# Linear-attention output product as seven block products behind the attention, with the final product begun in part

## Chip, cores and metric

The kernel runs on one core of a Trainium2 chip. The metric is the device time of one execution in microseconds; 1779.88 is the median of three runs before the change (1779.48 to 1781.68). Engines are named as in the profile: PE is TensorE (PEld its weight loads), DVE VectorE, ACT ScalarE, POOL GpSimd, SP the queue from which the transfers are issued.

## What is computed

One layer of a streaming encoder, 1024 tokens of width 1024, float32. Cut to what matters here:

```
h = rms_norm(x, pre_mix_norm)
h_q, h_k, h_v, h_g, h_a, c_q, c_kv, k_pe = split(h @ w_in)
o   = rms_norm(gated_linear_attention(h_q, h_k, h_v, h_a)) * silu(h_g)
y_a = o @ w_o_gla                       # the output product of the change
y_b = mla(c_q, c_kv, k_pe) @ w_o_mla    # the merge product
g_a, g_b = split(sigmoid(h @ w_gate + b_gate))
mixed = (g_a * y_a + g_b * y_b) @ w_out # the final product
x = x + rms_norm(mixed, post_mix_norm)
x = x + rms_norm(swiglu_ffn(rms_norm(x, pre_ffn_norm)))
```

## The kernel before

Everything is kept transposed: features on the 128 partitions, tokens along the free dimension in two halves of 512. A matmul in float32 is done as three (`mm3`, L93 to L96): each operand is split into a high half (cast, ACT, L104) and the rest (subtraction, DVE, L105), and high x high, high x low and low x high are added in PSUM. Weights come through `wload`: a transfer into a raw buffer (12 of them), then the split into wh and wl (7 of each). Activations come through `load4`: a transfer into a small buffer (15 of 128x512, tag h), then the split into one large buffer (34 of 128x1024, tag u).

The large products (projections, merge, FFN) are made by `wino`, the Strassen-Winograd form: of the 2x2 blocks of both operands seven block products instead of eight, with sums of operand blocks ahead (`t_ops`, `spilled_ops` for activations, `prep` for weights) and sums of products behind. Of some groups the first product and the second are made early and the first is spilled (npre groups, p1D).

Order of the work around the change. The attention (`qk`, `pt`, `av`) runs head by head over four blocks of 256 queries: scores p_sc, softmax on DVE and ACT, transposes p_pt, split into th and tl, product p_av; the scores of one step stand before the transposes of the step before. In the last head, parts of `gla_out(0, ...)` stand between them: the output product y_a for the first half of the tokens, eight tiles of 24 matmuls each (p_wog), each multiplied by its gate (L909) and stored to maD. The rest of `gla_out(0)` is interleaved with `merge_ops`, which makes the merge operands from omD (seven sets of four, 28 large buffers; b11 and b21 by `half0_ops`). Then comes the merge (p_pre, p_wa, p_wb, four of its groups begun early), whose `merge_use` multiplies by the second gate, adds maD for the first half and stores to mgD. Then `half_out(0)`, the final product for the first half (p_wout); then `gla_out(1)`, the output product for the second half, with `merge1` adding mgD and making the operands mp; then `half_out(1)`; then the FFN (p_pre, p_wa, p_wb again). The norm chain of the first half (`chain0`, with `pre_ffn`) runs beside `gla_out(1)` and `half_out(1)` and makes the FFN's first operands.

The order is written out in Python by generators that are advanced step by step; within this the framework's scheduler places instructions on each engine by priority in program order, and each engine then runs its list in order. So the SP queue: a transfer that waits holds those behind it.

Of the kernel before, what the change touches and what calls it, by code (L numbers as in the profile page):

```python
# [14 lines left out]
F32 = mybir.dt.float32  # L15
# [49 lines left out]
def body(tc, a, out):  # L65
# [139 lines left out]
    ogD = dp.tile([8, P, 1024], F32, name="ogD")  # L205
    gaD = dp.tile([8, P, 1024], F32, name="gaD")
    maD = dp.tile([8, P, H2], F32, name="maD")
# [232 lines left out]
    def wino(ops, slot, groups, npre):  # L440
# [56 lines left out]
        def full(gi, d, nxt, side):  # L497
# [3 lines left out]
            def banks():  # L501
                if gi % 2:
# [112 lines left out]
    def down_sums():  # L615

        for p in range(4):
            for c in range(0, KH * P, H2):
# [9 lines left out]
                yield 1  # L628

# [195 lines left out]
    def og_use(m0, m1):  # L825
        o = {}

        def load(i):
            o[i] = Hf("o")
            dma(o[i], oD[(m0, m1)[i // 2]][:, HS[i % 2]])  # L830

        def use(i, src):
# [4 lines left out]
            dma(ogD[(m0, m1)[i // 2]][:, HS[i % 2]], t)  # L837
# [5 lines left out]
    hgroups += [("wg", m, m + 1, og_use(m, m + 1)) for m in range(0, 8, 2)]  # L843
# [11 lines left out]
    sums = down_sums()  # L855
    for hd in range(HEADS_A):
# [15 lines left out]
        for i in range(NT + 2):  # L872
            run(sgen)
            run(fill)
            if 1 <= i < 7:
# [23 lines left out]
    def gla_out(j, ogs, use):  # L899
        for m in range(8):  # L900
            w = wload(a["wog"][m])
            ga = Hf("ga")
            dma(ga, gaD[m][:, HS[j]])
            ps = B(name="p_wog")
            for kt in range(KD):
                mm3(ps, w[kt], ogs[kt], kt == 0, kt == KD - 1)
                if kt == 3:
                    yield 1
            dve.tensor_tensor(ga, ps, ga, op=ALU.mult)  # L909
            use(m, ga)  # L910
            yield 1
# [128 lines left out]


# [10 lines left out]
    for s, (hd, blk) in enumerate(steps):  # L1052
# [22 lines left out]
    mops = dict(b11=[], b21=[], b22=[], t1=[], t2=[], t3=[], t4=[])  # L1075
    def merge_ops():
        ptt = pt(pend[1], pend[2])
        yield 1
        av(pend[0], pend[1], ptt)
        yield 1  # L1080
        yield from spilled_ops(mops, omD)

    mgen = merge_ops()
    def half0_ops():
        for n, k0 in (("b11", 0), ("b21", 4)):
            for kt in range(k0, k0 + 4):
                mops[n].append(load4(omD[kt][:, HS[0]]))
                if kt % 2:
                    yield 1

    h0gen = half0_ops()
    for i, _ in enumerate(gout):
        run(mgen)
        if i >= 6:
            run(h0gen)
    finish(h0gen)

    def merge_use(m0, m1):

        def use(i, src):  # L1100
# [3 lines left out]
            if j == 0:  # L1104
                ma = Hf("ma")
                dma(ma, maD[m])
            dve.tensor_tensor(gb, src, gb, op=ALU.mult)
            if j == 0:
                dve.tensor_tensor(gb, gb, ma, op=ALU.add)
# [3 lines left out]
    early, rest, _ = wino(mops, 0, [("wom", m, m + 1, merge_use(m, m + 1)) for m in range(0, 8, 2)], 4)  # L1113
    for _ in early:
        run(mgen)
    finish(mgen)
    rest()

    def half_out(j, wname, acts, sl, nk, filler=None, mid=None):

        raw = [U([P, 2, H2], name="raw") for _ in range(4)]
        sq = Hf("sq")
        for m in range(8):
            ps = B(name="p_" + wname)
            for k0 in range(0, nk, 4):
                k1 = min(nk, k0 + 4)
                w = wload(a[wname][m][:, k0 * P:k1 * P])
                for kt in range(k0, k1):
                    mm3(ps, w[kt - k0], cols(acts[kt], sl), kt == 0, kt == nk - 1)
                if mid is not None:  # L1130
                    run(mid)
# [48 lines left out]
    ogs = []  # L1180
# [324 lines left out]
```

## Time and profile before

| what | value |
|---|---|
| median of 3 runs | 1779.88 us |
| profiled execution | 1780.31 us, span 1778.5 us |
| PE busy | 1733.6 us, 8818 matmuls |
| DVE busy | 1268.2 us |
| ACT busy | 809.9 us |
| SP queue | 303.88 MB, 51.1% of 16 engines |
| granted clock | 0.997 |

The time of the profiled execution is the span and what lies around it. Busy times add the spans of instructions, which overlap on PE and DVE; how often an instruction can follow another is read from starts. A row of the timeline or of the chain gives the start, the length, and how many were merged (x24); a row of waits gives who waited for whom, the sum, how often, and the longest.

### The profile page before, as it was taken

Reading aid. Unit: us, or ns where it says so; the run is one execution under the profiler, and the core shown is the slowest. Engines: PE = TensorE matmul, PEld = TensorE weight load, DVE = VectorE, ACT = ScalarE, POOL = GpSimd, SP = SyncE. Lnnn points to the kernel's source line nnn. Section 1 sums busy time; section 2 is a strip of 40 time slices with the busy share of each in tenths; the row PEclk is TensorE's granted clock in tenths of the full one; section 3 lists DMA queues with packets and bytes.
Section 4 is the critical chain, followed back from the end, with each engine's and each line's share of the span. In section 5 each row is a group of like instructions: output and inputs, shape, how many; then the busy total and the mean of one; then the engine's idle time right before and its main releaser. Section 6 shows DMA issues by size and latency. Waiting matters only on the chain.

```text
span 1778.5 us, 25162 instructions
## 1 busy us (share of the span) xinstructions
PE 1733.6 (97%) x8818; PEld 1465.0 (82%) x8818; DVE 1268.2 (71%) x2275; ACT 809.9 (46%) x1511; POOL 39.5 (2%) x49
## 2 busy tenths in 40 slices
PE   8999999999999999999999999999999999999997
PEld 6889998777788898998877788788888888878886
DVE  7676665796556788787697668677887866655666
ACT  5485445634344554555452545452322322454542
POOL 0100000000000000000000000000000000000001
PEclk9999999999999999999999999999999999999999
DMA  6356753785556211112487654735554523593665
GB/s 243 137 197 204 226 169 121 272 283 195 182 197 206 60 51 53 34 51 94 169 307 271 210 184 142 243 135 173 177 183 153 186 95 109 175 317 108 197 187 172
DMA packets 172591, 305.49 MB, mean 172 GB/s; under 512 B 20080, under 2 KB 39280, under 8 KB 172464
## 3 DMA queue, kind: packets, MB, share of 16 engines
q1 hardware_dynamic: 172464, 303.88, 51.1%
q8 instruction: 69, 1.13, 0.3%
q14 instruction: 58, 0.48, 0.1%
HBM read 212.32 MB, written 89.39 MB: 170 GB/s over the span
## 4 chain that ended last, share of the span: by engine, by line
PE 84%; DMA 5%; DVE 5%; ACT 3%; issue 2%; SPq 1%; POOL 0%; DVEq 0%; ACTq 0%; POOLq 0%
PE p_wb L96 15%; PE p_wa L96 14%; PE p_wfd L96 11%; PE p_pre L96 8%; PE p_v L96 5%; PE p_wog L96 5%; PE p_wout L96 5%; PE p_sc L96 4%; PE p_av L96 3%; PE p_q L96 2%; PE p_k L96 2%; PE p_wqn L96 2%; PE p_pt L1013 1%; PE p_nrm L96 1%; DMA cl<-crD 1%
## 5 line engine op out<-in xcount | busy, mean ns | idle before, releaser
L104 ACT CAST wh<-raw 128x512 fp32r<-128x512 f32 (+1 forms) x335 | 200.7, 603 | 373.4 <-PE p_wfd L96 98.5
L105 DVE TENSOR_TENSOR wl<-raw,wh 128x512 fp32r<-128x512 f32 (+1 forms) x335 | 220.5, 664 | 160.3 <-ACT wh L104 152.5
L96 PE MATMUL p_wa<-t,wh 128*128 128x512 f32 x640 | 201.1, 394 | 3.9 <-DVE u L520 3.9
L96 PE MATMUL p_wb<-t,wh 128*128 128x512 f32 x640 | 198.2, 390 | 1.3 <-ACT wh L104 1.3
L96 PE MATMUL p_wfd<-ld,wh 128*128 128x512 f32 (+1 forms) x660 | 193.1, 377 | 3.0 <-ACT raw L1411 1.4
L96 PEld LDWEIGHTS p_wa<-t,wh 128*128 128x128 f32 x640 | 118.8, 188 | 33.4 <-DVE u L520 8.8
L96 PEld LDWEIGHTS p_wfd<-ld,wh 128*128 128x128 f32 x660 | 120.8, 188 | 26.7 <-ACT raw L1411 1.8
L96 PEld LDWEIGHTS p_wb<-t,wh 128*128 128x128 f32 x640 | 120.4, 188 | 26.6 <-ACT wh L104 1.7
L96 PE MATMUL p_wb<-t,wl 128*128 128x512 f32 x320 | 124.8, 390 | 0.0
L96 PE MATMUL p_wa<-t,wl 128*128 128x512 f32 x320 | 124.4, 391 | 0.0
L96 PE MATMUL p_wfd<-ld,wl 128*128 128x512 f32 (+1 forms) x330 | 123.2, 375 | 0.0
L104 ACT CAST wh<-sa 128x512 fp32r<-128x512 f32 x80 | 48.5, 620 | 156.8 <-DVE sa L458 82.9
L96 PE MATMUL p_v<-wh,hn 128*128 128x256 f32 x512 | 99.2, 283 | 0.6 <-ACT cr L667 0.5
L104 ACT CAST wh<-sb 128x512 fp32r<-128x512 f32 x80 | 49.7, 621 | 99.6 <-PE p_wb L96 49.3
L96 PEld LDWEIGHTS p_v<-wh,hn 128*128 128x128 f32 x512 | 82.5, 191 | 3.8 <-ACT cr L667 1.0
L96 PE MATMUL p_wog<-ld,wh 128*128 128x512 f32 x256 | 80.4, 392 | 1.0 <-DVE ld L105 0.7
L96 PE MATMUL p_pre<-b,wh 128*128 128x512 f32 x256 | 79.4, 396 | 0.0
L105 DVE TENSOR_TENSOR ld<-ld,ld 128x512 fp32r<-128x512 f32 x109 | 70.4, 687 | 9.8 <-ACT ld L104 9.6
L96 PE MATMUL p_v<-wl,hn 128*128 128x256 f32 x256 | 72.4, 283 | 0.0
L104 ACT CAST ld<-ld 128x512 fp32r<-128x512 f32 x109 | 63.4, 618 | 19.4 <-DMA ld<-fD 6.5
L96 PEld LDWEIGHTS p_wfd<-ld,wl 128*128 128x128 f32 x330 | 62.1, 188 | 11.3
L96 PE MATMUL p_pre<-hn,wh 128*128 128x512 f32 x224 | 71.0, 397 | 0.3 <-ACT p L485 0.2
(349 smaller groups left out, 4063.8 us busy)
## 6 DMA issues: line engine op xcount, KB each, us to landing
ld<-fD SPq DMA_DIRECT2D x77, 256.0 KB, 4.2
raw<-in_wfd_dram SPq DMA_DIRECT2D x60, 256.0 KB, 2.9
raw<-in_wfg_dram SPq DMA_DIRECT2D x60, 256.0 KB, 3.7
raw<-in_wfu_dram SPq DMA_DIRECT2D x60, 256.0 KB, 3.0
raw<-in_wgate_dram SPq DMA_DIRECT2D x48, 256.0 KB, 3.9
fD<-sg SPq DMA_DIRECT2D x41, 256.0 KB, 2.1
p1D<-p SPq DMA_DIRECT2D x34, 256.0 KB, 3.2
p<-p1D SPq DMA_DIRECT2D x34, 256.0 KB, 3.8
```

The costliest lines, as they stand in the source:

```text
L96: pe.matmul(o, l, r, start=start, stop=stop, skip_group_check=skip)
L104: act.copy(h, src)
L105: dve.tensor_tensor(l, src, h.bitcast(F32), op=ALU.subtract)
L1013: pe.transpose(tp[:, jj, i * P:(i + 1) * P], prs[i][:, j * P:(j + 1) * P], ident)
```

## The change

Three arrays change: gD holds the seven operand sets of the output product, soD the sums of its weights, maD both token halves. `og_use` in the projection stage, now with feature blocks m and m+4 in a group, makes the operand sums beside the gated columns and stores all to gD. `out_sums`, run after `down_sums` in the scan's stage (eight steps per head instead of six), makes the weights' sums. `gla_out` becomes the seven products n = 0 to 6 over four tiles p each, with both token halves at once, and stands as a whole after the last head; the merge operands are made beside it from its seventh step on. The merge makes no product early (npre 0) and begins on the other banks of PSUM. `merge_use` adds maD for both halves. `half_out(0)` begins with the first four k of three tiles. The operands of `half_out(1)` are loaded from mgD during `half_out(0)`, and `chain0` runs beside `half_out(1)` alone.

```diff
+    def out_sums():
+        for p in range(4):
+            a11, a12, a21, a22 = [wraw(a["wog"][2 * p + i][:, HS[k]]) for i in range(2) for k in range(2)]
+            yield 1
+            dve.tensor_tensor(a22, a21, a22, op=ALU.add)
+            dve.tensor_tensor(a21, a11, a21, op=ALU.subtract)
+            dve.tensor_tensor(a11, a22, a11, op=ALU.subtract)
+            dve.tensor_tensor(a12, a12, a11, op=ALU.subtract)
+            for i, t in enumerate((a22, a11, a21, a12)):
+                dma(soD[i, p], t)
+            yield 1
...
-            dma(ogD[(m0, m1)[i // 2]][:, HS[i % 2]], t)
+            if i != 1:
+                dma(gD[(0, 1, 1, 6)[i], m0], t)
+            if i:
+                f[i] = t
+            if i == 1:
+                b11, b12, b21, b22 = [f.pop(k) for k in range(4)]
+                ta, tb = U([P, 2, H2], name="ta"), U([P, 2, H2], name="tb")
+                dve.tensor_tensor(ta[:, 1], b12, b11, op=ALU.subtract)
+                dve.tensor_tensor(tb[:, 0], b22, ta[:, 1], op=ALU.subtract)
+                dve.tensor_tensor(ta[:, 0], b22, b12, op=ALU.subtract)
+                dve.tensor_tensor(tb[:, 1], b21, tb[:, 0], op=ALU.subtract)
+                for k, x in ((2, tb[:, 0]), (3, ta[:, 0]), (4, ta[:, 1]), (5, tb[:, 1])):
+                    dma(gD[k, m0], x)
...
-            if 1 <= i < 7:
+            if 1 <= i < 9:
                 run(sums)
...
+        def use(p, i, src):
+            m, j = 2 * p + i // 2, i % 2
             ga = Hf("ga")
             dma(ga, gaD[m][:, HS[j]])
+            dve.tensor_tensor(ga, src, ga, op=ALU.mult)
+            dma(maD[m][:, HS[j]], ga)
...
+        for n in range(7):
+            ops, nxt = nxt, []
+            loader = out_set(n + 1, nxt) if n < 6 else iter(())
...
+            bank = x if n in (0, 1, 4, 6) else y
+            for p in range(4):
+                w = wload(weights(n, p))
+                for k in range(4):
+                    mm3(bank[p], w[k], ops[k], n in (0, 2, 4, 5) and k == 0, k == 3, n in (1, 3, 6))
+                run(loader)
+                yield 1
+                if n == 0:
+                    act.copy(p1[p], x[p])
+                elif n == 1:
+                    use(p, 0, x[p])
+                elif n == 2:
+                    dve.tensor_tensor(u2[p], y[p], p1[p], op=ALU.add)
...
+                else:
+                    dve.tensor_tensor(u2[p], x[p], u2[p], op=ALU.add)
+                    use(p, 1, u2[p])
+            finish(loader)
...
-        if hd == HEADS_B - 1:
-            if blk == 0:
-                ogs = [load4(ogD[kt][:, HS[0]]) for kt in range(8)]
-                gout = gla_out(0, ogs, lambda m, t: dma(maD[m], t))
-            run(gout, (0,1,2,2)[blk])
...
+        if hd == HEADS_B - 1:
+            run(oload)
...
+    for i, _ in enumerate(gla_out()):
+        if i == 1:
+            ptt = pt(pend[1], pend[2])
+        elif i == 2:
+            av(pend[0], pend[1], ptt)
+        elif i >= 6 and i % 2 == 0:
+            run(h0gen)
+            run(mgen)
+        elif i >= 6:
+            run(mgen)
...
-    early, rest, _ = wino(mops, 0, [("wom", m, m + 1, merge_use(m, m + 1)) for m in range(0, 8, 2)], 4)
+    _, rest, _ = wino(mops, 0, [("wom", m, m + 1, merge_use(m, m + 1)) for m in range(0, 8, 2)], 0, 1)
...
+            for i in range(3) if m == 0 and ahead else (m,) if m > 2 or not ahead else ():
+                part(i, 0)
+            part(m, 4)
...
-    for i, _ in enumerate(gla_out(1, ogs, merge1)):
-        if i % 2:
-            run(c0)
-    r1, s1 = half_out(1, "wout", mp, ALL, KD, None, c0)
+    def mid0():
+        while True:
+            for n in (1, 2, 1):
+                run(c0, n)
+                yield 1
+    r1, s1 = half_out(1, "wout", mp1, ALL, KD, None, mid0())
```

How the order moves. First place: PE in the last head, from the transposes of its first block of queries to the product with the values (p_pt transposes, p_av the product, p_wog the output product, p_sc the scores of a later block). Before:

```order
L1013 MATMUL p_pt_9240<-cst,pf_9098 128x128 x2
L96 MATMUL p_wog_9263<-ld_9140,wh_9251 128x512 x2
L96 MATMUL p_wog_9263<-ld_9140,wl_9252 128x512
...
L96 MATMUL p_wog_9263<-ld_9160,wh_9257 128x512
L96 MATMUL p_av_9276<-th_9245,v2h_8602 128x256
L96 MATMUL p_wog_9263<-ld_9160,wh_9257 128x512
```

and with the change:

```order
L1099 MATMUL p_pt_9314<-cst,pf_9207 128x128 x2
L96 MATMUL p_av_9323<-th_9319,v2h_8711 128x256
L96 MATMUL p_av_9323<-tl_9320,v2h_8711 128x256
L96 MATMUL p_av_9323<-th_9319,v2l_8712 128x256
...
L96 MATMUL p_sc_9338<-kp_6004,qs_8368 128x320
```

The thirteen matmuls of the output product that stood between the transposes and p_av are gone, and nothing stands in their place.

Second place: DVE where the merge operands are made (hb and t1 to t4: sums of merge operands and their low halves; ld: low halves of loaded operands; wl: low halves of weights; ga: gate multiplication; po: sums of products). Before, over the last tiles of the output product:

```order
L105 TENSOR_TENSOR wl_2211_9878<-raw_2209_9875,wh_2210_9877 128x512
L587 TENSOR_TENSOR t3_2161_9693<-hb_2152_9664,hb_2150_9660 128x512
L105 TENSOR_TENSOR wl_2214_9884<-raw_2212_9881,wh_2213_9883 128x512
L105 TENSOR_TENSOR b22_2162_9695<-hb_2152_9664,b22_2162_9695 128x512
L591 TENSOR_TENSOR hb_2150_9660<-hb_2150_9660,hb_2149_9658 128x512
L592 TENSOR_TENSOR hb_2152_9664<-hb_2152_9664,hb_2150_9660 128x512
L909 TENSOR_TENSOR ga_2159_9678<-p_wog_2160_9680,ga_2159_9678 128x512
```

and with the change, at the weights of the last tile of the fourth product (wl_2274):

```order
L986 TENSOR_TENSOR po_2126_9522<-p_wog_2197_9816,po_2126_9522 128x512
L593 TENSOR_TENSOR hb_2255_10018<-hb_2255_10018,hb_2253_10014 128x512
L105 TENSOR_TENSOR ld_2267_10070<-ld_2266_10068,ld_2267_10070 128x512
L597 TENSOR_TENSOR hb_2254_10016<-hb_2254_10016,hb_2255_10018 128x512
L105 TENSOR_TENSOR t2_2268_10075<-hb_2255_10018,t2_2268_10075 128x512
L105 TENSOR_TENSOR t3_2269_10078<-t3_2261_10044,t3_2269_10078 128x512
L105 TENSOR_TENSOR t1_2270_10081<-hb_2253_10014,t1_2270_10081 128x512
L105 TENSOR_TENSOR t4_2271_10085<-hb_2254_10016,t4_2271_10085 128x512
L105 TENSOR_TENSOR wl_2274_10092<-raw_2272_10089,wh_2273_10091 128x512
L105 TENSOR_TENSOR wl_2283_10124<-raw_2281_10121,wh_2282_10123 128x512
```

Before, weights for coming tiles stood ahead of most of the merge's work; now the weights of the fourth product's last tile stand behind that of three of its four row pairs, and with operand loads and sums of products between.

Third place: PE in the sixth product of the changed output product (four tiles p_wog_2195 to 2198; ld_2285, 2294, 2305, 2312 its four operands). Before, a tile ran through all its operands:

```order
L96 MATMUL p_wog_2160_9680<-ld_2026_9140,wh_2154_9668 128x512 x2
L96 MATMUL p_wog_2160_9680<-ld_2026_9140,wl_2155_9669 128x512
L96 MATMUL p_wog_2160_9680<-ld_2028_9145,wh_2154_9668 128x512 x2
L96 MATMUL p_wog_2160_9680<-ld_2028_9145,wl_2155_9669 128x512
L96 MATMUL p_wog_2160_9680<-ld_2030_9150,wh_2154_9668 128x512 x2
```

and with the change:

```order
L96 MATMUL p_wog_2197_9816<-ld_2294_10175,wl_2329_10316 128x512
L96 MATMUL p_wog_2198_9817<-ld_2285_10141,wh_2334_10343 128x512 x2
L96 MATMUL p_wog_2198_9817<-ld_2285_10141,wl_2335_10344 128x512
L96 MATMUL p_wog_2198_9817<-ld_2294_10175,wh_2334_10343 128x512 x2
L96 MATMUL p_wog_2198_9817<-ld_2294_10175,wl_2335_10344 128x512
L96 MATMUL p_wog_2195_9814<-ld_2305_10219,wh_2316_10259 128x512
L96 MATMUL p_wog_2196_9815<-ld_2305_10219,wh_2322_10287 128x512
```

All four tiles take the first two operands before any takes the third.

## Rows read from the trace of the kernel before

**Rows 1.** The page's head and its busy times.

```profile
span 1778.5 us, 25162 instructions
PE 1733.6 (97%) x8818; PEld 1465.0 (82%) x8818; DVE 1268.2 (71%) x2275; ACT 809.9 (46%) x1511; POOL 39.5 (2%) x49
```

**Rows 2.** Groups of instructions: matmuls of the output product; count, busy us, mean ns, idle before.

```profile
L96 PE MATMUL p_wog<-ld,wh 128*128 128x512 f32 x256 | 80.4, 392 | 1.0 <-DVE ld L105 0.7 <-DVE tl L105 0.3
...
L96 PE MATMUL p_wog<-ld,wl 128*128 128x512 f32 x128 | 50.1, 391 | 0.0
```

**Rows 3.** The chain that ended last, in order of time: start us, us, what.

```profile
856.31 1.20 PE p_pt L1013 x11
...
872.88 2.87 PE p_av L96 x24
875.75 20.86 PE p_wog L96 x92
...
990.23 39.30 PE p_wout L96 x171
```

**Rows 4.** PE's waits from 856.3 to 1000 us: total us, times, longest.

```profile
PE p_wa L96 <- DVE u L520: 1.4, 1, 1.4
PE p_wb L96 <- ACT wh L104: 1.3, 1, 1.3
PE p_wout L96 <- ACT ld L104: 1.2, 2, 1.0
PE p_pre L96 <- DVE wl L105: 1.2, 1, 1.2
PE p_pre L96 <- ACT p L485: 1.0, 2, 0.7
PE p_wout L96 <- DVE ld L105: 0.8, 1, 0.8
PE p_wog L96 <- DVE tl L105: 0.3, 1, 0.3
```

**Rows 5.** Busy time by stretch: us, PE, PEld, DVE, ACT, POOL, clock, DMA share, GB/s.

```profile
890.00:900.00 10.00, 10.00 (x46) 8.29 (x45) 9.83 (x18) 6.86 (x12) 0.00 (x0) 1.00 0.93 306
900.00:910.00 10.00, 8.84 (x40) 6.99 (x39) 8.98 (x15) 6.54 (x13) 0.00 (x0) 1.00 0.83 286
910.00:920.00 10.00, 9.73 (x43) 7.73 (x42) 10.00 (x18) 3.03 (x6) 0.00 (x0) 1.00 0.98 345
920.00:930.00 10.00, 8.01 (x34) 5.99 (x34) 9.05 (x16) 4.41 (x8) 0.00 (x0) 1.00 0.90 311
...
280.00:300.00 20.00, 19.14 (x107) 16.40 (x106) 10.31 (x19) 11.54 (x23) 0.70 (x1) 1.00 0.25 90
520.00:540.00 20.00, 20.00 (x93) 16.59 (x92) 12.50 (x19) 9.47 (x14) 0.72 (x1) 1.00 0.67 230
```

**Rows 6.** Timeline of DVE near 907 us: start us, us, instruction.

```profile
905.97 0.68 DVE L592 TENSOR_TENSOR hb<-hb,hb 128x512 f32<-128x512 f32 x1
...
908.98 0.69 DVE L105 TENSOR_TENSOR t<-hb,t 128x512 fp32r<-128x512 f32 x1
```

**Rows 7.** The page's costliest groups: the cast of a loaded operand.

```profile
L104 ACT CAST ld<-ld 128x512 fp32r<-128x512 f32 x109 | 63.4, 618 | 19.4 <-DMA ld<-fD 6.5
```

**Rows 8.** PE's waits from 564 to 1125 us: the attention products.

```profile
PE p_av L96 <- DVE tl L105: 1.7, 3, 0.8
```

**Rows 9.** Transfers issued from 870 to 990 us: count, KB, median us to landing.

```profile
hb<-omD SPq DMA_DIRECT2D x16, 256.0 KB, 5.0
```

**Rows 10.** Timeline of PE near 470 us: start us, us, instruction, idle before.

```profile
464.67 0.50 PE L96 MATMUL p_wa<-t,wh 128*128 128x512 f32 x1 [1.64 <-DVE u L520]
...
472.45 1.16 PE L96 MATMUL p_nrm<-cst,cl 128*128 128x2 f32 x8 [1.37 <-DVE cl L643]
473.47 1.20 PE L96 MATMUL p_wa<-t,wh 128*128 128x512 f32 x2
```

**Rows 11.** Busy time by stretch, as in rows 5, after these two gaps.

```profile
474.00:476.00 2.00, 2.00 (x6) 1.57 (x5) 1.94 (x4) 1.23 (x3) 0.97 (x1) 0.50 0.00 0
```

More of the change, by code (lines that the diff above doesn't have):

```diff
@@ L204, in body @@
     oD = dp.tile([8, P, 1024], F32, name="oD")
-    ogD = dp.tile([8, P, 1024], F32, name="ogD")
+    gD = dp.tile([7, 4, P, H2], F32, name="gD")
+    soD = dp.tile([4, 4, P, H2], F32, name="soD")
     gaD = dp.tile([8, P, 1024], F32, name="gaD")
-    maD = dp.tile([8, P, H2], F32, name="maD")
+    maD = dp.tile([8, P, 1024], F32, name="maD")
     mgD = dp.tile([2, 8, P, H2], F32, name="mgD")
@@ L825, in og_use @@
     def og_use(m0, m1):
-        o = {}
+        o, f = {}, {}
         def load(i):
@@ L830, in load @@
             dma(o[i], oD[(m0, m1)[i // 2]][:, HS[i % 2]])
+            if i == 1:
+                f[0] = Hf("f11")
+                dma(f[0], gD[0, m0])
         def use(i, src):
@@ L842, in body @@
     hgroups += [("wgate", m, m + 1, gate_use(m, m + 1)) for m in range(0, 16, 2)]
-    hgroups += [("wg", m, m + 1, og_use(m, m + 1)) for m in range(0, 8, 2)]
+    hgroups += [("wg", m, m + 4, og_use(m, m + 4)) for m in range(4)]
     hpre, hrest, hflush = wino(hops, 0, hgroups, HPRE)
@@ L854, in body, with all_sums @@
     ggen = spilled_ops(hops, hnD)
-    sums = down_sums()
+    def all_sums():
+        yield from down_sums()
+        yield from out_sums()
+    sums = all_sums()
     for hd in range(HEADS_A):
@@ L896, in body, with out_set, gla_out, weights @@
         finish(x)
-    def gla_out(j, ogs, use):
-        for m in range(8):
-            w = wload(a["wog"][m])
+    osets = []
+    def out_set(n, res):
+        for p in range(4):
+            res.append(load4(gD[n, p]))
+            yield 1
+    oload = out_set(0, osets)
+    def gla_out():
+        def weights(n, p):
+            if n in (0, 1, 5):
+                return a["wog"][2 * p + (n == 5)][:, HS[n > 0]]
+            return soD[{2: 1, 3: 2, 4: 0, 6: 3}[n], p]
+        def use(p, i, src):
+            m, j = 2 * p + i // 2, i % 2
@@ L902, in gla_out, with halves @@
             ga = Hf("ga")
             dma(ga, gaD[m][:, HS[j]])
[L904 to L911, printed above, removed]
+            dve.tensor_tensor(ga, src, ga, op=ALU.mult)
+            dma(maD[m][:, HS[j]], ga)
+        def halves():
+            t = [U([P, 2, H2], name="po") for _ in range(2)]
+            return [t[p // 2][:, p % 2] for p in range(4)]
@@ L1039, in prep_all, with half0_ops @@
             yield from head_prep(2 * pr + 1)
+    mops = dict(b11=[], b21=[], b22=[], t1=[], t2=[], t3=[], t4=[])
+    def half0_ops():
+        for n, k0 in (("b11", 0), ("b21", 4)):
+            for kt in range(k0, k0 + 4):
+                mops[n].append(load4(omD[kt][:, HS[0]]))
+                if kt % 2:
+                    yield 1
+    h0gen = half0_ops()
+    mgen = spilled_ops(mops, omD)
     need = {}
@@ L1072, in body @@
         pend = cur
[L1075 to L1096, printed above, removed]
+        if hd == HEADS_B - 1:
+            run(oload)
     def merge_use(m0, m1):
@@ L1179, in body @@
     mp = [load4(mgD[0, m]) for m in range(8)]
[L1180 to L1181 removed]
+    mp1 = []
+    r0, s0 = half_out(0, "wout", mp, ALL, KD, lambda m: mp1.append(load4(mgD[1, m])), None, True)
     b11, b21 = [], []
```

62 lines of the change are left out of this document (37 added, 25 removed).

## Prediction

> **What bounds the kernel now.** I read the page's head first [rows 1]. TensorE (PE) is busy 97% of the span and VectorE (DVE) 71%, so a product that needs fewer matmuls should pay on PE, unless DVE is full where it stands. So the next views were of that place: the output product's matmuls [rows 2], the chain of work around the last attention head [rows 3], PE's waits there [rows 4] and the busy time by stretch [rows 5].
>
> Rows 2 count 384 matmuls of 128x512. Their price is their pace, not their span of about 390 ns, since they overlap: 92 in 20.86 us in [rows 3] make 0.2267 us each. I call the 12 matmuls of one output tile in one product a block: 2.72 us.
>
> Let T be the moment at which the last head's last scores are done and its last transposes begin, 856.31 us [rows 3]. From there to 990.23, where the final product runs without gaps, PE does 513 matmuls of this size (156 of the output product, 336 of the merge, 21 of the final product), 116.3 us, and the last two steps of attention (26 transposes at 1.20/11, 42 attention products at 2.87/24), 7.9 us. That is 124.2 of 133.9 us, an **excess of 9.7 us**. Seven of these are waits that can be seen [rows 4]: the seven rows sum to 7.2, most of them for DVE or for the ACT casts that work with it. Rows 5 say why: from 890 to 930 DVE is busy 9 to 10 us in every 10, and DMA 0.83 to 0.98. This stretch, in which the merge operands are made, is bound by DVE, and the change puts its work exactly there.
>
> DVE's price is again a pace: two instructions five apart begin at 905.97 and 908.98 us [rows 6], 0.602 us each, while the span of one is 0.69. The Trainium skill's VectorE: DVE Perf Modes, section "The DRAIN you can't avoid", lets the next instruction begin only when the pipe has emptied. By that the 60 instructions counted below would take 60 x 0.69 = 41.4 us instead of 36.1, and the result would be 5.3 us later. Rows 6 show the overlap in the very stretch, and I keep 0.602.
>
> **The change, part by part.**
>
> *Fewer matmuls.* Seven products of 48 matmuls replace 384: 48 fewer, 48 x 0.2267 = **-10.9 us**.
>
> *Last head.* Five half tiles (60 matmuls) that stood between its scores and its attention products leave. In the first order fence, PE now goes from the transposes of a block of queries straight to products that read their two halves, made by ACT and DVE. Without cover that is about 1.3 us (a cast of 0.62 [rows 7] and a subtraction of 0.69) in each of two early steps, later steps having scores beside them. From below, all three such waits seen in attention from 564 us on make 1.7 us, the longest 0.8 [rows 8]. I take **1.5**, ends 0 and 3.
>
> *The output product in the making of the merge operands.* From the last scores' maximum to the first operand of the final product, DVE has 242 rows in the new order and had 171: 71 x 0.602 = 42.7 us more, beside 180 more matmuls (40.8 us). Over the whole stage DVE still fits (146 of some 160 us). It does not fit at the front. In DVE's order the first gate multiplication (L954) needs the first block of the second product. PE reaches that after the 7.9 us of attention and 60 matmuls, T + 21.5, and DVE ends it at T + 22.1. Up to the weights of block 16 (the last of the fourth product) 60 instructions follow (second order fence: the merge operands of three of four row pairs stand before it). 60 x 0.602 = 36.1, so T + 58.2 at best. One of the merge loads stands on the SP queue behind the store of the second gate product, which is ready at T + 25.7; the load takes 5.0 us [rows 9], so its reader runs at T + 30.8 where DVE would come to it at T + 27.5: 3.3, and 0.6 for the second gate multiplication itself, makes T + 62.1. PE without waits would want these weights (third matmul of block 16) at 7.9 + 15 x 2.72 + 0.5 = T + 49.2. PE is **12.9 us late**, 9.0 if the load is no hindrance. I take 12.9, since loads of this kind took 5.0 us in just this traffic.
>
> After that 154 matmuls are left (34.9 us), and DVE, with 48 instructions before the last operand, keeps ahead in sum. But the 34 large buffers hold 28 merge operands and 4 partial sums by then, so two are left for the operands of the sixth and seventh products. Third order fence: PE runs the first two k for all four blocks, and the third operand waits for a buffer. Each time this costs a cast and a subtraction (about 1.3 us) less the 0.68 us of the three matmuls beside them; with hand-over I take 0.9, twice, **1.8**, ends 0 and 4. The stage ends at T + 62.1 + 34.9 + 1.8 = T + 98.8; without waits T + 84.1. **Excess 14.7.**
>
> *A gap of this length and the clock.* PE stood idle 1.64 us up to 464.67 and 1.37 us up to 472.45 [rows 10], and then the granted clock fell to 0.50, the 1.2 GHz level [rows 11]. From 473.47 eight matmuls ran at about 0.43 us each, 8 x 0.2 = 1.6 us lost. Gaps of 1.3 and 1.4 us [rows 4] left the clock at 1.00. I take one drop, **1.6**, ends 0 and 6.4 (four).
>
> *The merge.* It makes all seven products at once now. Per group (19.0 us of PE) DVE has 24 instructions, 14.4 us, and both halves load a partial sum. Its two waits of 1.3 and 1.4 [rows 4] I leave, **2.7**, ends 0 and 6. The stores and loads of the spilled first products (8 transfers) go; nothing waited on them but 1.0 us [rows 4], part of the old excess.
>
> *Final product begun in part.* The first halves of three tiles (8.2 us) run while the last four operands are loaded and split; before, PE waited 2.0 us here [rows 4]. I take **1.0**, ends 0 and 2.
>
> *Second half of the final product without the output product between.* The norm chain of the first half has 47 us instead of 90. Its first factor arrives about 13 us in (two tiles, 10.9 us, and the norm's own steps); then DVE has 51 instructions to the last operand that the FFN's first block needs, 30.7 us, some 1 us for 16 longer ones, and 1.5 us for the second norm: some 46 of 47. I take **0.5**, ends 0 and 3.
>
> *Earlier stages.* 16 sums of output-gate columns and 16 of weights, 9.6 us of DVE each, with some 50 more transfers. The gate columns lie where DVE is busy 12.5 of 20 us, the weight sums where it is 10.3 of 20 and DMA 0.25 [rows 5]. Covered: **0**, up to 2 if the scan's chain finds a sum before it.
>
> **Sum.** -10.9, -9.7 of old excess, and +1.5 + 14.7 + 1.6 + 2.7 + 1.0 + 0.5 = +22.0: +1.4 us on the profiled execution's 1780.31, whose span is 1778.5. It lies 0.4 above the median of the runs, so against that I forecast **1781.3 us: no change** (within 0.2%, 3.6 us, about what a measurement of this kernel can tell). This case's own range is 1776.3 to 1783.4.
>
> **Rivals.**
>
> *DVE's front-loading is absorbed: faster.* If PE finds other ready blocks, or the loads come early, the lag at block 16 is 9.0, without buffer waits and without a drop of the clock: 3.9 + 1.8 + 1.6 = 7.3 us less, 1774.0. For it: before, DVE was as full from 890 to 930 and PE lost only 3.4 us of 40 [rows 5]. Against: the engine executes in order, and PE's old blocks there did not each need an operand and a sum. Chance 0.30.
>
> *The clock falls again and again: slower.* Each gap in front of blocks 16, 21, 25 and in the last head drops the clock, four times 1.6 instead of once: +4.8, and PE then also feeds DVE's sums late by about 1 us: 1786 to 1787. It decides once the stage holds more than two stretches below 1.00. The Trainium skill's TensorE: Matmul & The Clock Gate, section "HAM oscillation — how this bites in real kernels", has the array return to half rate after idle gaps, so that every gap is paid twice; rows 10 and 11 agree for one pair of gaps, and [rows 4] has gaps of like size that cost nothing more. Chance 0.20.
>
> *DMA becomes the bound: slower.* Some 87 transfers of 0.262 MB (22.8 MB) stand on the SP queue from the last scores to the last operand of the seventh product, wanted by about T + 88: a rate under 259 GB/s would decide. Rows 5 show 286 to 345 in the four full stretches, so it has room, unless stores waiting for DVE hold the queue. At 240 GB/s it is 95 us, +7: 1788. Chance 0.10.
>
> *The saving is not there because the short norm chain makes the FFN wait the full 3 us:* 1784, in the slower part; this is in the forecast's upper bound and I give it no chance of its own.
>
> **How the numbers follow.** No change 0.40, faster 0.30, the two slower ones 0.30. The range 1773 to 1788 takes in the faster case with 1 us to spare and the clock and DMA cases, and leaves out what lies beyond, where several bounds would have to meet, some 2 in 10.
>
> **What would show it.** Right: 336 matmuls named p_wog; DVE busy over 9.5 of 10 us for some 40 us; a PE wait of 5 us or more for wl or a wait on the operands (ld) near 60 us after the last scores; the interval from the last scores to the final product near 180 us (98.8 + 1.6 + 76.2 + 2.7 + 1.0); the FFN's first product about 1.4 us later than before. Wrong: PE idle in the stage under 8 us in sum (faster), the granted clock at 0.5 in several stretches there, or DVE standing idle behind DMA for more than 8 us.

## The result, and the profile after the change

The change makes the kernel slower: 1831.12 us against 1779.68 us, a ratio of 1.0283 (95% interval 1.0265 to 1.0301). The forecast was 1781.3 with a range up to 1788; the time lies 43 us above it. The page's head after the change, to set beside [rows 1]:

```profile
span 1829.4 us, 25257 instructions
...
PE 1739.5 (95%) x8770; PEld 1460.7 (80%) x8770; DVE 1305.4 (71%) x2335; ACT 816.5 (45%) x1523; POOL 40.7 (2%) x49
```

The 48 matmuls are gone (8818 to 8770). What PE waits for is new; the first rows of PE's waits over the whole span:

```profile
PE p_wkn L96 <- DVE qr L1025: 16.2, 2, 14.9
PE p_qp L96 <- ACT cnh L104: 10.1, 1, 10.1
PE p_wog L96 <- DVE wl L105: 9.5, 1, 9.5
PE p_k L96 <- ACT wh L104: 5.3, 1, 5.3
PE p_wout L96 <- ACT ld L104: 4.4, 2, 3.9
```

p_k is the start of the kernel and was there before. The third and fifth rows lie where the prediction looked; the two largest waits lie 300 us earlier, between the projections and the attention. Starts read from PE's timeline share out the 50.9 us of span (T is the end of the last scores, as in the prediction):

| stretch | before | after | difference | predicted |
|---|---|---|---|---|
| start to the scan's last transposes | 327.0 | 332.4 | +5.4 | 0 (earlier stages) |
| to the first p_qp (attention's preparation) | 250.1 | 258.7 | +8.7 | 0 |
| to the first scores | 16.6 | 37.4 | +20.7 | 0 |
| to T | 262.6 | 256.2 | -6.4 | -6.7 |
| T to the FFN's first product | 263.9 | 284.6 | +20.7 | +8.1 |
| from there to the end | 658.3 | 660.1 | +1.8 | 0 |

(Before the change 36 matmuls of the output product stood before T, 8.2 us: with the 1.5 of the last head that makes the predicted -6.7. The rest of the sum is +8.1.) So 34.8 us are lost before the first scores, where the forecast had 0, and 12.6 more than forecast between T and the FFN. One profiled execution stands behind each column, and a stage that nothing touches can differ by some 3 us between executions (the experiments' table below).

**Before the first scores.** The first five loads of the attention (cnf, the normalized latents) moved. Their view, with durations, first and last start, in the kernel before:

```profile
L917 SPq DMA_DIRECT2D cnf<-cnD x5: 319/385/430, 466.7 to 536.5; - x5
```

and after the change:

```profile
L1003 SPq DMA_DIRECT2D cnf<-cnD x5: 382/408/448, 586.2 to 603.3; - x5
```

The timeline of the SP queue there (start us, us), and its longest wait:

```profile
585.12 1.04 SPq L868 DMA_DIRECT2D gD<-tb  x2
586.22 1.92 SPq L1003 DMA_DIRECT2D cnf<-cnD  x4
602.25 0.33 SPq L110 DMA_DIRECT2D raw<-in_wqn_dram  x1
602.91 0.33 SPq L110 DMA_DIRECT2D raw<-in_wkn_dram  x1
603.34 0.38 SPq L1003 DMA_DIRECT2D cnf<-cnD  x1
```

```profile
SPq L110 <- DVE wl L105: 14.3, 2, 14.0
```

They stand right behind the last operand sums' stores (gD<-tb). The fifth, and the rotary tables after it, then stand behind a weight load that waits 14.0 us for a raw buffer. DVE frees it with the rest of a weight split (L105), which comes behind ACT's cast, and that cast waits 6.54 us for p_qp. So the second wait, 14.9 us, follows from the first, 10.1. PE stood idle twice, and each time the granted clock fell to its lower level (0.50 is 1.2 GHz; a mean between 0.50 and 1.00 holds both levels); busy time by stretch, columns as in [rows 5]:

```profile
585.00:595.00 10.00, 3.81 (x8) 2.61 (x9) 3.62 (x5) 3.13 (x3) 0.00 (x0) 0.55 0.85 305
...
605.00:615.00 10.00, 0.00 (x0) 0.00 (x0) 1.50 (x2) 2.10 (x2) 0.00 (x0) 0.57 0.88 256
615.00:620.00 5.00, 2.86 (x6) 1.82 (x6) 4.47 (x8) 1.59 (x3) 0.00 (x0) 0.50 0.00 0
620.00:640.00 20.00, 18.57 (x112) 16.42 (x112) 15.01 (x37) 10.72 (x23) 0.00 (x0) 1.00 0.21 57
```

**The output stage.** The wait for the weights of block 16 that the prediction named is there, at 951.76, which is T + 67.1 (PE's timeline, then the busy time by stretch):

```profile
951.76 0.79 PE L96 MATMUL p_wog<-ld,wl 128*128 128x512 f32 x1 [9.49 <-DVE wl L105]
```

```profile
935.00:945.00 10.00, 6.57 (x25) 4.01 (x24) 9.98 (x17) 6.86 (x13) 0.00 (x0) 0.97 1.05 386
945.00:950.00 5.00, 0.00 (x0) 0.00 (x0) 5.00 (x10) 2.18 (x4) 0.00 (x0) 0.50 0.06 22
950.00:955.00 5.00, 3.24 (x8) 2.60 (x9) 5.00 (x9) 1.24 (x2) 0.00 (x0) 0.54 0.37 111
```

DVE is full for 20 us while DMA falls to 0.06: DVE alone is late. The stage's last p_wog ends at T + 109.6.

**The final product.** PE ends the merge at 1070.69 and begins p_wout at 1074.58. The end of the chain of waits there (start us, us, what):

```profile
1067.50 4.26 DMA ma<-maD
1071.76 0.52 DVE gb L1177
...
1074.26 0.32 SPq L1178
...
1074.62 5.03 DMA ld<-mgD
1079.67 0.63 ACT ld L104
1080.34 0.76 PE p_wout L96
```

and the timeline of SP's queue and the busy time by stretch beside it:

```profile
1067.50 0.43 SPq L1175 DMA_DIRECT2D ma<-maD  x1
...
1071.02 0.43 SPq L613 DMA_DIRECT2D ld<-mgD  x1
...
1074.62 2.40 SPq L613 DMA_DIRECT2D ld<-mgD  x5
```

```profile
1075.00:1080.00 5.00, 4.88 (x10) 2.63 (x9) 1.58 (x3) 1.56 (x3) 0.00 (x0) 0.50 0.87 288
```

All eight operands are loaded after the last gate and partial-sum load (1067.50), the first of them at 1071.02, behind a store of the merge (mgD) that waits 2.6 us for DVE. So the part that was to run ahead has nothing to run on.

### The profile page after: what moved, and what is told of

Same layout as the page of the kernel before. It is cut to its first block, busy times and chain, and to the rows that moved or that the text cites. A ratio compares the mean times of both kernels' runs of the same rounds, so it can differ in the third digit from the quotient of the medians.

```text
span 1829.4 us, 25257 instructions
## 1 busy us (share of the span) xinstructions
PE 1739.5 (95%) x8770; PEld 1460.7 (80%) x8770; DVE 1305.4 (71%) x2335; ACT 816.5 (45%) x1523; POOL 40.7 (2%) x49
## 5 line engine op out<-in xcount | busy, mean ns | idle before, releaser
L104 ACT CAST wh<-raw 128x512 fp32r<-128x512 f32 (+2 forms) x331 | 198.0, 603 | 357.7 <-PE p_wfd L96 96.0
L105 DVE TENSOR_TENSOR wl<-raw,wh 128x512 fp32r<-128x512 f32 (+2 forms) x331 | 217.0, 663 | 155.3 <-ACT wh L104 150.8
L105 DVE TENSOR_TENSOR ld<-ld,ld 128x512 fp32r<-128x512 f32 x129 | 84.5, 687 | 21.9 <-ACT ld L104 21.7
L104 ACT CAST ld<-ld 128x512 fp32r<-128x512 f32 x129 | 76.3, 618 | 49.7 <-DMA ld<-gD 16.9
L96 PE MATMUL p_wout<-ld,wh 128*128 128x512 f32 x256 | 81.7, 401 | 4.4 <-ACT ld L104 4.4
L96 PE MATMUL p_wog<-ld,wh 128*128 128x512 f32 x224 | 73.6, 405 | 5.6 <-DVE ld L105 1.8
```

The costliest lines, as they stand in the source:

```text
L96: pe.matmul(o, l, r, start=start, stop=stop, skip_group_check=skip)
L104: act.copy(h, src)
L105: dve.tensor_tensor(l, src, h.bitcast(F32), op=ALU.subtract)
```

## The experiments

All kernels beside one another. Ratios are to the kernel before on the same chip, with 95% intervals; the other columns are us of the profiled execution (first p_qp, first scores, T, last p_wog of the stage, FFN's first product).

| kernel | ratio | p_qp | scores | T | p_wog | FFN | T to FFN |
|---|---|---|---|---|---|---|---|
| before | 1 | 577.1 | 593.7 | 856.3 | | 1120.2 | 263.9 |
| the change | 1.0283 (1.0265-1.0301) | 591.2 | 628.5 | 884.7 | 994.3 | 1169.3 | 284.6 |
| e1 | 1.0141 (1.0118-1.0163) | 584.3 | 602.1 | 858.2 | 969.2 | 1146.0 | 287.8 |
| e2 | 1.0285 (1.0262-1.0308) | 588.8 | 627.0 | 883.1 | 995.0 | 1171.3 | 288.2 |
| e3 | 1.0272 (1.0253-1.0290) | 593.0 | 632.4 | 888.6 | 993.9 | 1168.5 | 279.9 |
| e4 | 1.0292 (1.0263-1.0321) | 594.9 | 635.8 | 891.9 | 1003.9 | 1179.6 | 287.7 |
| e5 | 1.0146 (1.0131-1.0161) | 584.7 | 625.6 | 888.4 | | 1151.6 | 263.2 |
| e6 | 1.0024 (1.0010-1.0038) | 587.7 | 604.3 | 867.0 | | 1133.9 | 266.9 |
| e7 | 1.0124 (1.0107-1.0141) | 587.6 | 605.5 | 861.7 | 966.4 | 1146.9 | 285.2 |
| e8 | 1.0050 (1.0035-1.0066) | 583.7 | 601.5 | 857.7 | 962.0 | 1127.3 | 269.6 |
| e9 | 1.0038 (1.0025-1.0051) | 578.6 | 596.4 | 852.7 | 952.0 | 1126.4 | 273.7 |
| e10 | 1.0012 (1.0001-1.0024) | 579.0 | 596.9 | 853.2 | 954.9 | 1123.5 | 270.3 |
| e11 | 1.0050 (1.0035-1.0065) | 585.9 | 603.8 | 860.1 | 965.8 | 1135.7 | 275.6 |
| e12 | 0.9992 (0.9981-1.0003) | 580.2 | 598.0 | 854.3 | 949.2 | 1117.3 | 263.0 |
| e13 | 1.0038 (1.0025-1.0051) | 574.6 | 592.4 | 848.7 | 948.5 | 1124.0 | 275.3 |

Stages that an experiment doesn't touch differ by some 3 us between profiled executions (T to FFN is 284.6 in the change, 287.7 to 288.2 in e1, e2 and e4), and the projections by up to 9 (249 to 258 us where no loads are late). So the ratio decides on the whole, and a stage's time only where it moves by more. e7 and e8 stand on e1 and e3 together, a kernel that was not run by itself; what they add is judged against the stages of e1 and e3.

### e1: sums in place

```diff
-                ta, tb = U([P, 2, H2], name="ta"), U([P, 2, H2], name="tb")
-                dve.tensor_tensor(ta[:, 1], b12, b11, op=ALU.subtract)
...
+                dve.tensor_tensor(b11, b12, b11, op=ALU.subtract)
+                dve.tensor_tensor(b12, b22, b12, op=ALU.subtract)
+                dve.tensor_tensor(b22, b22, b11, op=ALU.subtract)
+                dve.tensor_tensor(b21, b21, b22, op=ALU.subtract)
```

> The changed kernel with the four operand sums of each output-gate group written into the 128x512 buffers that already hold the gated columns, so that og_use takes none of the 34 large buffers; the same DVE instructions and stores are issued. Theory (the large buffers are handed out in program order, so the attention's five latent loads cnf stand behind the last sums and came at 586 to 603 us instead of 467 to 537): the waits of 10.1 us before p_qp and 14.9 us before p_wkn and the stretch at half clock behind them go, first p_qp near 581 us, first scores near 600 us instead of 628, the whole 27 to 31 us faster than 1831, about 1802. Rival (the 16 sums and the extra stores fill DVE and the SP queue at the end of the projections): the loads stay late and the time stays within 5 us of 1831.

The ratio falls from 1.0283 to 1.0141, 25 us (27 to 31 were expected). The loads are back, with the same DVE work and stores:

```profile
L1002 SPq DMA_DIRECT2D cnf<-cnD x5: 319/382/430, 475.3 to 543.2; - x5
```

From p_qp to the scores it is 17.8 us, as before (16.6). The theory holds; the rival (work and bytes) falls.

### e5: the large buffers alone, in the kernel before

```diff
+            if i == 1:
+                ta, tb = U([P, 2, H2], name="ta"), U([P, 2, H2], name="tb")
+                dve.tensor_copy(ta[:, 0, 0:8], t[:, 0:8])
...
+                dma(xtD[m0 // 2, 0], ta[:, 0, 0:8])
...
```

> The kernel before with one thing of the change added: at each of the four output-gate groups' last products two large buffers are taken, 8 columns of them written by DVE and stored to memory; nothing is computed with them. Theory (large buffers are handed out in program order, so taking two there holds the attention's five latent loads cnf back behind the last group): the loads, issued at 467 to 537 us before, come after the last product of the projections, PE waits some 10 us before p_qp and some 15 us before p_wkn, and the kernel before becomes 23 to 30 us slower, about 1806. Rival (it is the sums' work and the stores' bytes that delay the loads): within 3 us of the kernel before.

1.0146 x 1780.92 us, 26 us slower, with the loads late and the waits of PE there:

```profile
L924 SPq DMA_DIRECT2D cnf<-cnD x5: 382/382/447, 579.5 to 597.3; - x5
```

```profile
PE p_wkn L96 <- DVE qr L946: 16.9, 2, 15.6
PE p_qp L96 <- ACT cnh L104: 8.7, 1, 8.7
```

With e1 this settles it from both sides: two large buffers per group, whatever is put in them, cost 25 to 26 us by the ratios.

### e2: weight sums out of the scan

```diff
-            if 1 <= i < 9:
+            if 1 <= i < 7:
                 run(sums)
...
+        if gi >= 3:
+            calls[0] += 1
+            if calls[0] % 6 == 0:
+                run(osums)
```

> The changed kernel with the sums of the output weights (out_sums, eight steps) taken out of the scan and run in the projections, one step every six block products from the fourth group on. Theory (these sums stand between the scan's own DVE steps and delay its chain): the scan's last transposes end near 327 us instead of 332, the waits of p_o fall from 6.3 to about 3 us, the whole 3 to 6 us faster, about 1826. Rival (the scan is late for another reason, such as the transfers): within 2 us of 1831.

The ratio does not move, so on the whole the edit gains nothing that can be seen. For the scan the theory holds. It ends here at 329.7 us, in the change at 332.4 (PE's timeline, the last transposes, in the change and here):

```profile
331.81 0.60 PE L778 MATMUL p_oT<-cst,osc 128*128 128x128 f32 x4
```

```profile
329.12 0.60 PE L778 MATMUL p_oT<-cst,osc 128*128 128x128 f32 x4
```

All the kernels part in the same way: the six with the weight sums in the scan (the change, e1, e3, e4, e7, e8) end it at 332.3 to 335.1 us, the six with the sums moved (e2, e9 to e13) at 325.6 to 329.7, and the three that don't have them (before, e5, e6) at 327.0 to 329.4. p_o waits 6.3 us in its three rows in the change, 4.3 here, 3.1 before.

### e3: merge operands spread

```diff
-        elif i >= 6 and i % 2 == 0:
-            run(h0gen)
-            run(mgen)
-        elif i >= 6:
+        elif i >= 4 and i % 2 == 0:
             run(mgen)
+        elif i >= 9 and i % 4 == 1:
+            run(h0gen)
```

> The changed kernel with the making of the merge operands spread evenly: one of its twelve steps at every second block of the output product from the fifth to the 27th, the four steps of the first-half operands at the 10th, 14th, 18th, 22nd and 26th, instead of a step at each block from the seventh on. Theory (DVE's work fits the stage in sum and is only too dense in front of block 16): the wait of 9.5 us for the weights of that block goes, with the low clock behind it; from the last scores to the last p_wog 97 to 101 us instead of 109.6; the whole 8 to 13 us faster, about 1820. Rival 1 (DVE's sum is the bound): the wait moves to the end of the stage, within 4 us of 1831. Rival 2 (transfers are the bound): waits on loaded operands instead, within 4 us of 1831.

The 9.5 us wait is gone, and T to FFN is 5 to 8 us shorter; the ratios do not separate. From T to the last p_wog it is 105.3 us, where 97 to 101 was expected and the change has 109.6. Most of what is left stands in the sixth and seventh products, as waits for operands and for the large buffers that the partial sums (po) hold:

```profile
PE p_wog L96 <- ACT ld L104: 3.9, 4, 1.5
PE p_wog L96 <- DVE po L995: 3.2, 1, 3.2
PE p_wog L96 <- DVE ld L105: 2.0, 2, 1.3
PE p_wog L96 <- DVE wl L105: 1.1, 1, 1.1
```

So the order in front of block 16 made that wait, but less than half of its length was to be had by this order.

### e4: early loads of four operands

```diff
+    def side2(gi):
+        if gi == 3:
+            late[0] += 1
+            if late[0] >= 3 and len(mp) < 4:
+                mp.append(load4(mgD[0, len(mp)]))
```

> The changed kernel with the first four operands of the final product loaded inside the last group of the merge, one after each of its third to sixth products, instead of behind its last gate loads. Theory (the loads stand on the SP queue behind the last group's eight gate and partial-sum loads because small buffers are handed out in program order, so the part of the final product that was to run first has no operands): the 3.9 us wait before the first p_wout and the stretch at half clock behind it (2.5 us) go, 4 to 7 us faster, about 1825. Rival (the loads are late because the large buffers are still held by merge operands): the wait moves to the merge or stays, within 2 us of 1831.

No gain. The first p_wout now begins before the merge ends. But the last three gate loads, which had started 179.4 us after T (at 1064.09 in the change), went behind x loads and start 186.4 us after T (T is 891.9 here), and the loads of the other four operands come behind them: PE waits 4.1 us for these, 48 matmuls into the product (timeline of the SP queue, PE's waits):

```profile
1076.99 1.34 SPq L1241 DMA_DIRECT2D xr<-in_xT_dram  x1
1078.38 0.42 SPq L1173 DMA_DIRECT2D gb<-gbD  x1
```

```profile
PE p_wout L96 <- ACT ld L104: 4.1, 1, 4.1
```

### e8: all of the first half's operands early, two of them without memory (on e1 and e3)

```diff
+            if m0 == 6 and j == 0:
+                mpl.extend(op4([gb], "mp"))
+            else:
+                dma(mgD[j, m], gb)
...
+            for _ in range((0, 0, 0, 2, 2, 2, 0, 0)[late[0]]):
+                mp.append(load4(mgD[0, len(mp)]))
```

> The changed kernel with the operand sums in place and the merge operands spread, and in addition the first six operands of the final product loaded inside the merge's last group, and the seventh and eighth split straight from the merge's results instead of through a store and a load. Without the addition 1799 to 1806. Theory (the wait of 4 us at the first p_wout is the trip of these operands through memory behind the last gate loads): wait and half clock go, 4 to 7 us faster, about 1797. Rival (as when four operands alone were loaded early: the last gate and partial-sum loads are pushed back by what is put ahead of them, and PE waits the same a product later): no gain.

1.0050. T to FFN is 269.6 us, against 279.9 in e3, and PE's waits from T to the FFN have no row of p_wout any more (5.0 us in e3, 4.4 in the change). So the late operands were the cause of the wait at the final product; four of them early (e4) was not enough. The edit does two things, six early loads and two operands without memory, and which of them it takes was not tried apart.

### e6: the final product begun in part, in the kernel before

The edit is `half_out` of the change in the kernel before, with `ahead` for the first half.

> The kernel before with the final product begun in part alone: the first four k of three tiles of its first half run before the other four k of the first tile. Theory (this part of the change is sound where its operands are there; before, PE waited 2.0 us at this place for the last operands): 0.5 to 2 us faster. Rival (the operands of the first k are no earlier than the others, since all eight loads are issued together behind the last gate loads): within 0.5 us.

No gain: p_wout still waits 1.8 us (1.3 and 0.5; 2.0 in [rows 4]), as the rival says. That the kernel is 0.24% slower (4 us, where the rival had 0.5) has no shown cause. Its profiled execution, the slowest of twelve, is 10.6 us late at the first p_qp, long before the edit (the last section), so this trace can't tell it.

### e7: the merge operands' sums on POOL (on e1 and e3)

```diff
-    mgen = spilled_ops(mops, omD)
+    mgen = spilled_ops(mops, omD, pool)
```

> The changed kernel with the operand sums in place (as in e1_sums_in_place) and the merge operands spread (as in e3_spread_merge_operands), and in addition the 16 sums of merge operands moved from DVE to POOL (GpSimd), which stands idle there. The two former changes should add to 1799 to 1806. Theory (DVE's density bounds the stage): 16 x 0.60 = 9.6 us less on DVE make the waits before the sixth and seventh product smaller, 3 to 8 us faster than that, about 1797. Rival 1 (large buffers and loads bound what is left): no gain, 1799 to 1806. Rival 2 (a POOL sum, 0.73 us for half the size, takes 1.4 us or slows DVE while it runs, and four stand in a chain): 2 to 6 us slower than without.

1.0124: the time lies in the 1799 to 1806 that e1 and e3 alone were expected to take, so no gain is seen. T to the last p_wog is 104.7 us (105.3 in e3), and the merge behind it 82 (76 in e3). The timelines of POOL and of DVE at the same time (start us, us):

```profile
905.06 2.17 POOL L588 TENSOR_TENSOR t<-hb,hb 128x512 f32<-128x512 f32 x1 [9.16 <-PE p_wog L96]
907.31 1.62 POOL L592 TENSOR_TENSOR hb<-hb,hb 128x512 f32<-128x512 f32 x1
...
911.92 1.62 POOL L597 TENSOR_TENSOR hb<-hb,hb 128x512 f32<-128x512 f32 x1
```

```profile
906.25 1.52 DVE L105 TENSOR_TENSOR ld<-ld,ld 128x512 fp32r<-128x512 f32 x1 [0.19 <-ACT ld L104]
907.70 0.68 DVE L983 TENSOR_TENSOR po<-p_wog,po 128x512 f32<-128x512 f32 x1
...
911.21 3.48 DVE L105 TENSOR_TENSOR ld<-ld,ld 128x512 fp32r<-128x512 f32 x3
```

A sum takes 1.6 to 2.2 us on POOL in these rows, and beside it a DVE subtraction of two SBUF tiles takes 1.52 us, three of them 3.48, where one takes 0.69 alone; the one that reads PSUM (po, beside POOL's 907.31) keeps its 0.68.

### e9, e10, e11: buffers and the queue (on e8, with e2)

e9 makes the first-half operands later, e10 in addition issues the stores of the gated product from POOL's queue, e11 is e10 without e9's lateness.

```diff
-        elif i >= 9 and i % 4 == 1:
+        elif i in (11, 17, 25, 27):
             run(h0gen)
...
-            dma(maD[m][:, HS[j]], ga)
+            pool.dma_start(maD[m][:, HS[j]], ga)
```

> The kernel with the direct operands (sums in place, merge operands spread, final product's operands early), and in addition the output weights' sums moved from the scan to the projections, and the eight large buffers of the merge's first-half operands filled later: at the 12th, 18th, 26th and 28th block instead of the 10th, 14th, 18th and 22nd. Without these two 1792. Theory (what is left in the output stage are waits for large buffers in the sixth and seventh products: 1.6 us on ld, 3.2 us on the partial sums whose buffers the last operands take): four buffers more are free there, the two waits and the half clock behind them shrink by 4 to 7 us; the scan ends 2 to 5 us earlier; the whole at 1781 to 1787, within 0.4% of the kernel before. Rival (DVE, 97 of 115 us busy in this stage, bounds it whatever the order): the waits only move, and no more than the scan's 2 to 4 us are gained, 1788 to 1791.

> The same kernel with the 16 stores of the gated output product issued from POOL's queue instead of SP's. On SP these stores waited 29 us in sum for DVE's gate multiplications, with the loads queued behind them. Theory (the loads of the coming products are late because they stand behind stores that wait): waits on loaded operands in the output stage shrink by 2 to 5 us more, 1777 to 1784. Rival 1 (DVE bounds, the loads come in time): no gain, within 2 us of the kernel without this edit. Rival 2 (this queue's transfers cost more than SP's): 2 to 10 us slower.

> The kernel with the stores on POOL's queue, with the merge's first-half operands made again at the 10th, 14th, 18th and 22nd block. Making them late had moved 6.4 us of waiting to the merge's first product. Theory (those operands must be there when the merge begins, and the stores on another queue make the loads early): from the last scores to the FFN's start 265 to 268 us instead of 270.3, the time 1778 to 1783, within 0.2% of the kernel before or up to 0.3% faster. Rival (the large buffers are then full again in the sixth and seventh products): waits of 3 to 5 us there, the time 1783 to 1788.

In e9 the last p_wog comes 5 us sooner than in e8, but a wait of 6.4 us before the merge's first p_wb takes it back: T to FFN 273.7, and the time is the rival's. The waits of its SP queue and of PE:

```profile
SPq L957 <- DVE ga L956: 28.7, 16, 3.8
```

```profile
PE p_wb L96 <- ACT wh L104: 6.4, 1, 6.4
```

e10, on the same chip, is 6.1 us faster by the medians (1784.71 and 1790.84), 4.6 by the ratios. The stores' 28.7 us are gone from SP, and so is the wait before p_wb. But PE's waits on loaded operands, which the theory was about, did not shrink (3.4 us on ld, 2.5 in e9; 5.0 on po, 1.6 in e9), and in e13, with the same queue, the wait before p_wb is back. So the gain is there and its way is not shown. e11 misses: 3.2 us on po and 4.6 on ld, 1791.41, and its projections took 7 us longer. e10 is the best kernel of the change, 0.12% above the kernel before; none beats it.

### e12: 16 DVE sums left out (on e11)

```diff
-    mgen = spilled_ops(mops, omD)
+    mgen = spilled_ops(mops, omD, False)
```

> The same kernel as e11_queue_without_late with the 16 sums of merge operands left out of the computation: the split takes unsummed blocks, so DVE has 16 x 0.60 = 9.6 us less in the output stage; transfers, buffers and TensorE's work stay. Theory A (DVE's sum bounds the stage): from the last scores to the last output product 5 to 9 us less than with the sums. Theory B (large buffers and loads bound it): within 2 us of it.

Theory A, and more than its 5 to 9: T to the last p_wog is 94.9 us instead of 105.7, and the medians of the same chip are 1781.06 and 1791.41. Against e10, which has the better order, T to FFN is 7 us shorter and the ratio 0.2% lower. So 16 instructions, 9.6 us of DVE, are worth 4 to 10 us of the kernel. The kernel leaves the sums out, so it is no version to use; with them goes a small buffer (t3) of each row pair and the chain of three sums ahead of the splits, which this run doesn't part from DVE's time.

### e13: the same work where DVE stood idle (on e10)

```diff
-        elif i >= 4 and i % 2 == 0:
+        if i in (2, 3, 5, 6, 8, 9, 12, 14, 16, 22, 25, 26):
             run(mgen)
```

> The kernel with the stores on POOL's queue, with the merge operands' twelve steps put where DVE had room: six of them in the first ten blocks, where DVE was busy 2.5 to 4 of every 5 us, three up to the 17th block, three in the last six; the first-half operands at the 11th, 19th, 25th and 28th. Theory (DVE's work in the stage, some 142 instructions of 0.60 us, bounds it, and what DVE stands idle at the front is lost): from the last scores to the last output product 96 to 99 us instead of 101.8, the time 1779 to 1783, the kernel before or 0.2% under it. Rival (in the first blocks the loads are not there earlier, DMA being full from 20 us after the last scores on, so the work moved to the front waits and delays the weights behind it): a new wait for weights in the second to fourth product and 1785 to 1792.

T to the last p_wog is 99.8 us, 2 less than in e10 (96 to 99 was expected), but the merge's first p_wb then waits 6.5 us, T to FFN is 5 longer, and the time, 1789.63, is the rival's. Of the orders tried for the merge operands each moved the waits; leaving work out (e12) made them less.

## Why the prediction was wrong, by its steps

- **Fewer matmuls, last head.** Right: 48 fewer, and -6.4 us from the first scores to T against -6.7 (so close an agreement is in part luck, since untouched stages differ by some 3 us).
- **Earlier stages: 0, up to 2.** This step failed, by 34.8 us. It asked whether DVE and DMA had room for 16 sums and 50 transfers, and did not ask which buffers the sums take. The pool gives its large buffers out in program order, so eight new ones ahead of the attention hold back its first loads; e1 and e5 show 25 to 26 us of it. The scan's 5.4 us go with the weight sums in it (e2): there the prediction named the way, a sum before the scan's chain, and gave it at most 2, where the kernels that have them there end the scan on average some 5 us later. The few us that are left are no more than executions differ by. The prediction made the same count of buffers for the sixth product, and there only.
- **The output product in the making of the merge operands.** The mechanism was right, its size not. The weights of block 16 came at T + 67 (T + 62.1 forecast). The first gate multiplication began at T + 24.3, not ended at T + 22.1: DVE stood idle 3.84 us ahead of it for a loaded operand (DVE's timeline):

```profile
906.11 0.69 DVE L105 TENSOR_TENSOR ld<-ld,ld 128x512 fp32r<-128x512 f32 x1 [3.84 <-ACT ld L104]
...
909.00 0.68 DVE L954 TENSOR_TENSOR ga<-p_wog,ga 128x512 f32<-128x512 f32 x1
```

  The working took DVE to be full from the first gate multiplication on; from 905 to 925 it was busy 7.1 to 7.2 of 10 us, and it was full only from 935 to 965. PE waited 9.5 us, not 12.9, because it was itself 8 us late: the working priced all blocks ahead at full speed, and from 902 to 942 PE already waited 3.8 us and ran slower. The stage ends 9.2 us later than forecast (T + 109.6 against 98.8 + 1.6, with 1.8 us of merge matmuls in it): 5.0 of it before block 16's weights, the rest after.
- **One drop of the clock.** There was one in this stage (945 to 955), as forecast, but three more, at 585, 605 and 1075, behind gaps that were not.
- **Merge (2.7) and FFN (0.5).** About right: the merge took 76.4 us for 328 matmuls of 74.4, and the FFN did not wait.
- **Final product begun in part: 1.0.** Failed: 3.9 us idle and a stretch at half clock, 7.4 us in all up to 1080.34 (ten matmuls there, 2.3 us at full pace). The step took it that the last four operands are loaded while the first four are used; SP's order has all eight behind the last gate and partial-sum loads, and the change loads partial sums for both halves. e8 shows that the wait goes with the late operands.

Of the rivals, the clock that falls repeatedly came about in part, but outside the stage that it named. DMA as the bound did not: at the output stage's longest wait it stood at 0.06. But that rival's proviso, stores that wait for DVE and hold the queue, did come about: the stores of the gated product held SP 10.5 us from T to 930, and up to 955 DVE waited 10.0 us for loads (7.3 by way of ACT's casts of loaded operands, 2.7 for hb), more than the 8 that the prediction named as a sign against it.

## What to carry to other kernels

- A tile taken from a shared ring of buffers costs what the next takers in program order lose. When a change adds one, follow the pool to the first load behind it, and read the order of the transfer queue over the whole program, not only where the change is.
- Where DVE is full, trading 48 matmuls (10.9 us) for sums is no gain here: leaving 16 of its instructions out was worth 4 to 10 us (e12).
- A product begun early needs its operands' loads moved too; look for what stands ahead of them on the queue.

## What the runs showed of the hardware

- A DVE subtraction of two SBUF tiles beside a POOL sum is held up (e7: 1.52 us for 0.69), one that reads PSUM is not (0.68). The Trainium skill's SBUF — State Buffer, section "SBUF: two separate sides", names a port pair that DVE with two SBUF inputs and a GpSimd operation on SBUF share as an exclusive lock, held by whichever starts first for its whole instruction; the trace agrees with it (1.52 and 0.68 us).
- In the projections a short gap on PE was followed by a low clock in some executions and not in others. In e6, behind a gap of 2.27 us at 445:

```profile
445.00:450.00 5.00, 4.56 (x16) 3.91 (x17) 1.06 (x3) 0.00 (x0) 1.38 (x1) 0.60 0.16 52
450.00:455.00 5.00, 5.00 (x17) 3.92 (x17) 3.26 (x6) 2.04 (x4) 0.00 (x0) 0.72 0.01 2
```

  The gap before the same instruction was 0.73 us in the kernel before, and there the clock stayed at 1.00 from 400 to 460; in the change it was 1.24, and the clock 0.66 from 445 to 450. From the scan to p_qp the same code took 250.1 us in the kernel before and 258.3 in e6, 250.9 in e10 and 258.0 in e11; how much of that is gaps and how much is clock was not worked out.
- DMA moved 386 GB/s from 935 to 945 us in the change, loads and stores together, more than the 345 of [rows 5].
